# First values of a decoder trunk from unsplit float32 products, with g_mix transposed ahead of x

## The chip, the core and the metric

The kernel runs on one core of a Trainium2 chip. The metric is device time in microseconds (us), the median of several executions; lower is better. A difference counts here when it is over 0.2% of the time, 0.69 us.

## The reference, cut to what matters

One layer of a decoder trunk works on 256 rows x of 1024 floats, all in float32: a mixer with four head groups (a, b, c, d), a cross-attention into 256 memory rows (mem), a squared-ReLU MLP (1024 to 4096 to 1024) and a last RMSNorm.

```
h = rmsnorm(x, g_mix);  proj = h @ w_in            # w_in: 1024 x 2816
aq, ak, av, bq, bk, bv, cq, ck, cv, dq, dk, dv = split(proj)
y = concat(dilated(aq, ak, av), stick(bq, bk, bv), sliding(cq, ck, cv), moba(dq, dk, dv))
x = x + (group_norm(y) * g_group) @ w_out
x = x + cross_attention(rmsnorm(x, g_cross), rmsnorm(mem, g_mem))
x = x + square(relu(rmsnorm(x, g_mlp) @ w_up)) @ w_down
return rmsnorm(x, g_final)
```

The change touches the very first product, `av`: 256 rows times 256 columns of `w_in`, contracted over 1024.

## The kernel before

**Tiles.** The 256 rows are two blocks of 128, x0 and x1 (t = 0, 1). The 1024 features are eight blocks of 128 (k). A weight unit is 1024 x 256 and comes in two halves of 512 KB (k 0 to 3 and 4 to 7).

**Split products.** TensorE (PE) multiplies in the type that the rows call fp32r, so that an operand is split in two: ScalarE (ACT) copies it to the rounded form (hi, L314 for weights, L400 for activations) and VectorE (DVE) subtracts that from the whole (lo, L315, L401). A product then is three (hi·hi, hi·lo, lo·hi: L424 to L426). Weights land in four `raw` buffers; a raw buffer is free again when its L315 has run.

**The front.** SyncE (SP) loads x0, half 0 of av, x1, half 1 of av, then the units aq, ak and so on; ACT's queue loads g_mix, 8 x 128 floats (`grow`). PE multiplies a zero tile by itself 40 times (L366, the warm-ups). For each block of rows, `gained_T` transposes eight 128 x 128 pieces of x on PE (L407), DVE multiplies them by the gains gT (L417, into `tmp`) and the result is split into hThi (L400) and hTlo (L401). gT comes from one small transpose of g_mix (L375) and a copy (L376). `rstd_row` squares x with a sum on ACT (L392), DVE scales the sum (L385, `var`), and GpSimd (POOL) raises it to -1/2 (L386, `rstd`). The two rstd columns are spread over the partitions by two PE transposes (L459) and copied to rk and rq (L462, L463).

The values of group a are 48 products (L495): for each block of rows and each half of the features, hi·hi, lo·hi and hi·lo. After them on PE come the units aq and ak (48 products each, L424 to L426), the scores (L637), and all else. The bias strip of group a goes through DRAM: L471 (PE), L472 (DVE), a store (L473) and three broadcast loads (L717), both issued by POOL.

**Order.** The program is not issued as written. Each operation is handed to a planner (`Plan`) with an estimated price; the planner runs all engines forward on these prices, takes at each step the operation that it ranks highest among those that can start, and emits them in that order. So every engine works through a fixed queue, and an instruction that waits holds all behind it. A changed price or dependence can move instructions far from the change.

Of the kernel before, what the change touches and what calls it, by code (L numbers as in the profile page):

```python
# [11 lines left out]
F32 = mybir.dt.float32  # L12
# [6 lines left out]
P = 128  # L19
S = 256  # L20
D = 1024
KB = D // P
# [4 lines left out]
SPL = 15  # L27
# [4 lines left out]
FRONT = 20.0  # L32
EARLY = 1.0
NUDGE = 0.5
LAST = 2
SPLIT = 640
LASTC = 768
# [178 lines left out]
def trunk(ctx: ExitStack, tc: tile.TileContext, a: dict, out: bass.AP):  # L216
    nc = tc.nc
# [7 lines left out]
    def buf(tag, shape, dtype=F32, bufs=1, pool=sb):  # L225
        return Buf(plan, pool, shape, dtype, tag, bufs)

    def pst(n=1):
        return buf("ps", [P, 512], F32, 4, ps)

    def acct():
        return buf("acc", [P, 512], F32, 4, ps)


    def act(n, fn, r, w, aps=0):
        plan.add("ACT", 0.02 + n * 0.00093 + 0.1 * aps, fn, r, w)

    def dve(n, fn, r, w, rate=1.05):
        plan.add("DVE", 0.065 + n * rate * 1e-3, fn, r, w)
# [9 lines left out]
    def pe(cost, fn, r, w):  # L249
        plan.add("PE", cost, fn, r, w)  # L250

    def dma(nbytes, fn, r, w):
        plan.add("DMA", max(0.06, nbytes / 360e3), fn, r, w)
# [9 lines left out]
    def tsl(t):  # L263
        return slice(t * P, (t + 1) * P)

    def nsl(n):
        return slice(n * 512, (n + 1) * 512)
# [14 lines left out]
    units = {}  # L282
# [10 lines left out]
    def load(u, *which):  # L293

        n, c = units[u].shape[1] // 2, units[u].shape[2]
        got = parts.setdefault(u, ([], n))[0]
        for part in which or range(2):
            raw = buf("raw", [P, n, c], F32, RAW)
            hi, lo = buf("w", [P, n, c], F32R, SPL), buf("w", [P, n, c], F32R, SPL)
            dma(n * c * 512, lambda raw=raw, part=part: nc.sync.dma_start(raw.t, units[u][:, part * n:(part + 1) * n]), [], [raw])  # L300
            if u == "cq":
                def view(z, r):
                    return z.t[:, :, tsl(r)].rearrange("p k (g e) -> p k g e", g=2)

                def src(z, r):
                    return z.t.rearrange("p k (g r e) -> p k r g e", g=2, r=2)[:, :, r]

                for r in range(2):
                    act(512, lambda raw=raw, hi=hi, r=r: nc.scalar.activation(view(hi, r), src(raw, r), AF.Copy),
                        [raw], [(hi, r)])  # L310
                    dve(512, lambda raw=raw, hi=hi, lo=lo, r=r: nc.vector.tensor_sub(
                        view(lo, r), src(raw, r), view(hi, r).bitcast(F32)), [raw, (hi, r)], [(lo, r)])
            else:
                act(1024, lambda raw=raw, hi=hi: nc.scalar.activation(hi.t, raw.t, AF.Copy), [raw], [hi])  # L314
                dve(1024, lambda raw=raw, hi=hi, lo=lo: nc.vector.tensor_sub(lo.t, raw.t, hi.t.bitcast(F32)), [raw, hi], [lo])  # L315
            got.append((hi, lo))

    def wt(u, k):

        got, n = parts[u]  # L320
        return got[k // n], k % n


    xt = []
# [1 line left out]
        xt.append(buf(f"x{t}", [P, D]))  # L326

    def load_x(t):
        dma(P * D * 4, lambda: nc.sync.dma_start(xt[t].t, a["x"][0, tsl(t), :]), [], [xt[t]])

    GN = ("g_mix", "g_cross", "g_mem", "g_mlp")
    grow = [buf("grow0", [KB, P]), buf("grow1", [3 * KB, P])]
# [1 line left out]
    def load_gain(i, eng):  # L334
        j = max(i - 1, 0) * KB
        dma(4096, lambda: eng.dma_start(
            grow[i > 0].t[j:j + KB, :], a[GN[i]][0].rearrange("(k p) -> k p", p=P)), [], [(grow[i > 0], i)])

    load_x(0)
    load_gain(0, nc.scalar)  # L340
    load("av", 0)
    load_x(1)
    load("av", 1)
    ident, mhalf, warm = buf("ident", [P, P]), buf("mhalf", [P, 1]), buf("warm", [P, 512], BF16)
    pool(0.5, lambda: make_identity(nc, ident.t), [], [ident])
    pool(0.05, lambda: nc.gpsimd.memset(mhalf.t, -0.5), [], [mhalf])
# [48 lines left out]
    def pair(tag, n, bufs):  # L395
        return tuple(buf(tag + x, [P, n, S], F32R, bufs) for x in ("hi", "lo"))

    def split_to(hl, key, sl, src, view, n):
        hi, lo = hl
        act(n, lambda: nc.scalar.activation(hi.t[sl], view(), AF.Copy), [src], [(hi, key)])  # L400
        dve(n, lambda: nc.vector.tensor_sub(lo.t[sl], view(), hi.t[sl].bitcast(F32)), [src, (hi, key)], [(lo, key)])  # L401

    def transpose(dst, src, view, n, keys):

        def go():
            for k in range(n):
                nc.tensor.transpose(dst[:, tsl(k)], view()[:, tsl(k)], ident.t)  # L407
        pe(0.109 * n, go, [ident] + keys, [dst])

    def gained_T(x, g, hl, t):  # L410

        tmp = buf("tmp", [P, KB, P], F32, 3)
        for n in range(2):
            ks = slice(4 * n, 4 * n + 4)
            pt = pst()
            transpose(pt, x, lambda n=n: x[:, nsl(n)], 4, [(x, n)])
            dve(512, lambda ks=ks, pt=pt: nc.vector.tensor_tensor(  # L417
                tmp[:, ks, :], pt.t.rearrange("p (k t) -> p k t", k=4), gT[g > 0][:, max(g - 1, 0), ks, None].to_broadcast([P, 4, P]),
                op=ALU.mult), [pt, gT[g > 0]], [(tmp, n)])
            split_to(hl, (t, n), (slice(None), ks, tsl(t)), (tmp, n), lambda ks=ks: tmp[:, ks, :], 512)  # L420

    def mm3(dst, l, r, start, stop):
        (lh, ll), (rh, rl) = l, r
# [22 lines left out]


    h1 = pair("hT", KB, 2)
    r1 = []
    for t in range(2):  # L450
        gained_T(xt[t], 0, h1, t)
        r1.append(rstd_row(xt[t], lambda t=t: xt[t].t, D))

    rq, rk = buf("rq", [P, S]), buf("rk", [P, S])
# [21 lines left out]
    def project(gi):  # L476
        n = "abcd"[gi]
        q, k = buf("q", [P, 2, S], F32, 2), buf("k", [P, 2, S], F32, 2)
        names = (n + "q", n + "k" if gi != 2 else "ckv")
        v = buf("v4", [P, 2, 4, E + 1], F32, 2) if gi != 2 else buf("v2", [P, 2, 2, E + 1])  # L480
        pool(0.1, lambda: nc.gpsimd.memset(v[:, :, :, E:E + 1], 1.0), [], [(v, 0), (v, 1)])

        def values():
            if gi:
                load(n + "v")
            for t in range(2):
                pv = acct()
                if gi:
                    proj(pv, lambda pv=pv: pv[:, 0:256], n + "v", h1, t)
                else:  # L490
                    for half in range(2):
                        for p in ((0, 0), (1, 0), (0, 1)):
                            for kk in range(4 * half, 4 * half + 4):
                                w, j = wt("av", kk)
                                pe(0.109, lambda p=p, kk=kk, w=w, j=j, t=t, pv=pv: nc.tensor.matmul(  # L495
                                    pv[:, 0:256], h1[p[0]][:, kk, tsl(t)], w[p[1]][:, j], start=kk == 0 and p == (0, 0),
                                    stop=kk == KB - 1 and p == (0, 1)), [w[p[1]], (h1[p[0]], (t, half))], [pv])
                act(256, lambda t=t, pv=pv: nc.scalar.activation(
                    v[:, t, :, 0:E], pv[:, 0:256].rearrange("p (h e) -> p h e", h=4), AF.Copy, scale=r1[t].t),
                    [pv, r1[t]], [(v, t)], 1)  # L500

        if gi == 0:
            values()
        for u, z, r in zip(names, (q, k), (rq, rk)):
            if u != "aq":
                load(u)
            acc = acct()
            for i in range(2):
                proj_T(acc, lambda acc=acc, i=i: acc[:, i * S:(i + 1) * S], u, i, h1)
            dve(512, lambda z=z, r=r, acc=acc: nc.vector.tensor_tensor(  # L510
                z.t, acc.t.rearrange("p (i t) -> p i t", i=2), r[:, None, :].to_broadcast([P, 2, S]), op=ALU.mult),
                [acc, r], [z])
        if gi == 2:
            pt = pst()
            transpose(pt, k, lambda: k[:, 1, :], 2, [k])
            for t in range(2):
                act(128, lambda t=t: nc.scalar.activation(
                    v[:, t, :, 0:E], pt[:, tsl(t)].rearrange("p (g e) -> p g e", g=2), AF.Copy), [pt], [(v, t)])
        elif gi:
            values()  # L520
        return q, k, v
# [238 lines left out]
    for t in range(2):  # L760
        pv = pst()
# [12 lines left out]
    for t in range(2):  # L774
        plan.nudge = NUDGE * (1 - t)
        residual(pacc[t], t)
# [10 lines left out]
        w, nm = buf("w4", [P, 4, S], F32, 2), buf("nm", [P, 4], F32, 4)  # L787
# [62 lines left out]
    p = {}  # L850
# [114 lines left out]
    for f, i in enumerate(final):  # L965
        load(("down", i))
        if f < len(final) - LAST:
            for t in range(2):
                for acc, c0, c1 in pieces[t]:
                    rows_mm(acc, hid[i], ("down", i), t, c0, c1, f == 0 and acc not in p.values(), False)  # L970
    for t in range(2):
        o, x = buf("tmp", [P, KB, P], F32, 3), xt[t]
        ssq, pre, var = buf("ssq3", [P, 4], F32, 2), buf("ssq", [P, 1], F32, 4), buf("var", [P, 1], F32, 4)
        sq, r = buf("sq", [P, D], BF16, 1), buf("rstd", [P, 1], F32, 16)
        for c, (acc, c0, c1) in enumerate(pieces[t]):
            cs, n = slice(c0, c1), c0 // 512
            for i in final[-LAST:]:
                rows_mm(acc, hid[i], ("down", i), t, c0, c1, i == final[0] and acc not in p.values(), i == final[-1])
# [67 lines left out]
```

## Time and profile before

| | us |
|---|---|
| three runs | 342.67, 343.07, 343.04 |
| median | 343.04 |
| the profiled execution | 342.83 |
| its span, first to last instruction | 340.9 |

The profiled execution is 0.21 us under the median, and 1.93 us of it lie outside its span. PE is busy 97% of the span, DVE 88%, ACT 68%, POOL 8%. The views name an instruction by its line, engine and out<-in tiles; "busy" of PE includes a modelled end of each product, so that products that start 0.12 us apart are shown 0.28 us long.

### The profile page before, as it was taken

How to read it: one execution, taken by the hardware profiler on the slowest of the kernel's cores; microseconds unless marked ns; L12 is line 12 of the kernel's file. 1: busy time of each engine (PE TensorE's matmuls, PEld its weight loads, DVE VectorE, ACT ScalarE, POOL GpSimd, SP SyncE). 2: the span in 40 equal slices, each digit the busy share in tenths (PEclk: the TensorE clock that was granted, in tenths of full speed). 3: DMA queues.
4: the chain of work that ended last, by engine and by line, in shares of the span. 5: the costliest groups of instructions: out<-in, count | busy, mean ns of one | idle time of the engine just before them, and what ended most of it. 6: DMA issues, size and time to landing. Idle time of an engine off the chain costs nothing.

```text
span 340.9 us, 6081 instructions
## 1 busy us (share of the span) xinstructions
PE 329.0 (97%) x2326; PEld 302.4 (89%) x2326; DVE 299.2 (88%) x488; ACT 231.7 (68%) x371; POOL 27.6 (8%) x46
## 2 busy tenths in 40 slices
PE   7799999999999999999999999999999999999992
PEld 6699899999898789998998899888999889998882
DVE  3758779779998499878999999999999999999994
ACT  4578857369794476883885876778668678665822
POOL 6422000000121002200020000000000000000000
PEclk9999999999999999999999999999999999999997
DMA  7989775640137334847743646476566574644003
GB/s 257 317 254 330 218 201 181 236 137 0 64 109 214 112 122 147 268 143 227 268 139 109 222 160 232 147 229 198 178 225 211 178 248 159 212 123 125 3 0 123
DMA packets 39757, 59.88 MB, mean 176 GB/s; under 512 B 1990, under 2 KB 32896, under 8 KB 39728
## 3 DMA queue, kind: packets, MB, share of 16 engines
q1 hardware_dynamic: 38928, 57.49, 52.2%
q0 software_dynamic: 640, 1.80, 1.8%
q8 instruction: 18, 0.29, 0.4%
q10 hardware_dynamic: 160, 0.20, 0.2%
q14 instruction: 11, 0.09, 0.1%
HBM read 58.42 MB, written 1.07 MB: 175 GB/s over the span
## 4 chain that ended last, share of the span: by engine, by line
PE 57%; DVE 21%; ACT 7%; issue 7%; DMA 5%; POOL 1%; SPq 0%; POOLq 0%; ACTq 0%; DVEq 0%
PE ps L425 9%; PE ps L424 9%; PE ps L426 9%; PE acc L424 8%; PE acc L425 8%; PE acc L426 8%; DVE w L315 5%; DVE w L872 4%; DMA raw<-in_w_in_dram 3%; PE ps L557 3%; PE ps L407 3%; DMA x<-in_x_dram 2%; ACT w L314 2%; DVE tmp L878 2%; POOL rstd L386 1%
## 5 line engine op out<-in xcount | busy, mean ns | idle before, releaser
L315 DVE TENSOR_TENSOR w<-raw,w 128x1024 fp32r<-128x1024 f32 x72 | 86.1, 1218 | 11.6 <-ACT w L314 8.2
L314 ACT ACTIVATE w<-raw 128x1024 fp32r<-128x1024 f32 x72 | 73.9, 1053 | 14.8 <-PE acc L425 7.6
L425 PE MATMUL ps<-hTlo,w 128*128 128x256 f32 x256 | 72.1, 281 | 0.0
L424 PE MATMUL ps<-hThi,w 128*128 128x256 f32 x256 | 71.9, 281 | 0.0
L426 PE MATMUL ps<-hThi,w 128*128 128x256 f32 x256 | 71.8, 281 | 0.0
L424 PEld LDWEIGHTS ps<-hThi,w 128*128 128x128 f32 x256 | 48.2, 188 | 0.7
L425 PEld LDWEIGHTS ps<-hTlo,w 128*128 128x128 f32 x256 | 48.1, 188 | 0.6
L426 PEld LDWEIGHTS ps<-hThi,w 128*128 128x128 f32 x256 | 48.3, 189 | 0.0
L424 PE MATMUL acc<-w,yThi 128*128 128x512 f32 (+1 forms) x112 | 45.2, 404 | 0.0
L425 PE MATMUL acc<-w,yThi 128*128 128x512 f32 (+1 forms) x112 | 43.7, 390 | 0.0
L426 PE MATMUL acc<-w,yTlo 128*128 128x512 f32 (+1 forms) x112 | 43.7, 390 | 0.0
L871 ACT ACTIVATE w<-tmp 128x1024 fp32r<-128x1024 f32 x28 | 29.6, 1058 | 15.6 <-DVE tmp L881 13.1
L424 PE MATMUL acc<-hThi,w 128*128 128x256 f32 x128 | 36.6, 286 | 0.0
L425 PE MATMUL acc<-hTlo,w 128*128 128x256 f32 x128 | 36.1, 282 | 0.0
L426 PE MATMUL acc<-hThi,w 128*128 128x256 f32 x128 | 35.8, 280 | 0.0
L872 DVE TENSOR_TENSOR w<-tmp,w 128x1024 fp32r<-128x1024 f32 x28 | 34.1, 1218 | 0.0
L386 POOL TENSOR_TENSOR rstd<-var,mhalf 128x1 f32<-128x1 f32 x16 | 15.9, 998 | 137.5 <-DVE var L385 89.4
L426 PEld LDWEIGHTS acc<-w,yTlo 128*128 128x128 f32 x112 | 21.0, 188 | 5.0
L425 PEld LDWEIGHTS acc<-w,yThi 128*128 128x128 f32 x112 | 21.1, 188 | 4.2
L424 PEld LDWEIGHTS acc<-w,yThi 128*128 128x128 f32 x112 | 21.1, 188 | 4.0
L424 PEld LDWEIGHTS acc<-hThi,w 128*128 128x128 f32 x128 | 24.1, 188 | 0.4
L426 PEld LDWEIGHTS acc<-hThi,w 128*128 128x128 f32 x128 | 24.2, 189 | 0.0
(189 smaller groups left out, 708.6 us busy)
## 6 DMA issues: line engine op xcount, KB each, us to landing
raw<-in_w_up_dram SPq DMA_DIRECT2D x32, 512.0 KB, 4.2
raw<-in_w_in_dram SPq DMA_DIRECT2D x22, 512.0 KB, 4.9
hThi<-in_w_down_dram SPq DMA_DIRECT2D x14, 512.0 KB, 3.4
hTlo<-in_w_down_dram SPq DMA_DIRECT2D x14, 512.0 KB, 4.1
raw<-in_w_out_dram SPq DMA_DIRECT2D x8, 512.0 KB, 3.4
raw<-in_w_xkv_dram SPq DMA_DIRECT2D x4, 512.0 KB, 3.5
raw<-in_w_down_dram SPq DMA_DIRECT2D x4, 512.0 KB, 4.3
w<-dstrip POOLq DMA_DIRECT2D x3, 512.0 KB, 8.3
```

The source lines that it names most:

```text
L314: act(1024, lambda raw=raw, hi=hi: nc.scalar.activation(hi.t, raw.t, AF.Copy), [raw], [hi])
L315: dve(1024, lambda raw=raw, hi=hi, lo=lo: nc.vector.tensor_sub(lo.t, raw.t, hi.t.bitcast(F32)), [raw, hi], [lo])
L386: pool(0.5, lambda: nc.gpsimd.tensor_tensor(r.t, v.t, mhalf.t, op=ALU.pow), [v, mhalf], [r])
L407: nc.tensor.transpose(dst[:, tsl(k)], view()[:, tsl(k)], ident.t)
L424: nc.tensor.matmul(dst, lh, rh, start=start, stop=False)
L425: nc.tensor.matmul(dst, lh, rl, start=False, stop=False)
L426: nc.tensor.matmul(dst, ll, rh, start=False, stop=stop)
L557: nc.tensor.matmul(view()[:, h, :], z[:, i, :], v[:, j, kv(h), :], start=j == 0, stop=j == len(pT[h]) - 1)
L871: act(512 * n, lambda: nc.scalar.activation(hi.t, view(), AF.Copy), [key], [hi])
L872: dve(512 * n, lambda: nc.vector.tensor_sub(lo.t, view(), hi.t.bitcast(F32)), [key, hi], [lo])
L878: dve(1024, lambda: nc.vector.tensor_sub(s.t, raw[:, 1:2].to_broadcast([P, 2, 512]), raw[:, 0:4:3]), [raw], [s])
```

## The change

The unit av is loaded whole into two tiles of the weight pool (`whole`), not through `raw`, and is not split any more. `gained_T` hands back `tmp`, x transposed and multiplied by the gains in full float32, and the values are 16 products of it with `whole`, float32 by float32, instead of 48 split ones. The 2 copies L314 and 2 subtractions L315 of av are gone; x's own split stays, since aq and all later units use it. The load of g_mix is written first. The load of x1 is given a planned price 1.75 times as large, so that the planner thinks that it lands later; the load itself is the same.

```diff
+FULL = 0.43
     def load_x(t):
-        dma(P * D * 4, lambda: nc.sync.dma_start(xt[t].t, a["x"][0, tsl(t), :]), [], [xt[t]])
+        dma(P * D * (4 + 3 * t), lambda: nc.sync.dma_start(xt[t].t, a["x"][0, tsl(t), :]), [], [xt[t]])
...
+    whole = []
+
+    def load_whole(part):
+
+        whole.append(buf("w", [P, KB // 2, 256], F32, SPL))
+        dma(P * D * 4, lambda: nc.sync.dma_start(whole[part].t, units["av"][:, 4 * part:4 * part + 4]), [], [whole[part]])
+
+    load_gain(0, nc.scalar)
     load_x(0)
-    load_gain(0, nc.scalar)
-    load("av", 0)
+    load_whole(0)
     load_x(1)
-    load("av", 1)
+    load_whole(1)
...
             split_to(hl, (t, n), (slice(None), ks, tsl(t)), (tmp, n), lambda ks=ks: tmp[:, ks, :], 512)
+        return tmp
...
-    r1 = []
+    g1, r1 = [], []
     for t in range(2):
-        gained_T(xt[t], 0, h1, t)
+        g1.append(gained_T(xt[t], 0, h1, t))
...
-                    for half in range(2):
-                        for p in ((0, 0), (1, 0), (0, 1)):
-                            for kk in range(4 * half, 4 * half + 4):
-                                w, j = wt("av", kk)
-                                pe(0.109, lambda p=p, kk=kk, w=w, j=j, t=t, pv=pv: nc.tensor.matmul(
-                                    pv[:, 0:256], h1[p[0]][:, kk, tsl(t)], w[p[1]][:, j], start=kk == 0 and p == (0, 0),
-                                    stop=kk == KB - 1 and p == (0, 1)), [w[p[1]], (h1[p[0]], (t, half))], [pv])
+                    for kk in range(KB):
+                        pe(FULL, lambda kk=kk, t=t, pv=pv: nc.tensor.matmul(
+                            pv[:, 0:256], g1[t][:, kk, :], whole[kk // 4][:, kk % 4], start=kk == 0, stop=kk == KB - 1),
+                            [whole[kk // 4], (g1[t], kk // 4)], [pv])
```

The new order is seen best around the two spread transposes. PE before, from the middle of the values to the first product of aq (`acc_209` is the value sum of x1, `acc_194` that of x0, `rstd_248` belongs to x1, `acc_291` to aq):

```order
L495 MATMUL acc_209<-w_147,hTlo_204 128x256 x2
L495 MATMUL acc_209<-w_173,hThi_163 128x256 x3
L459 MATMUL ps_261<-ident_65,rstd_175 128x128
L459 MATMUL ps_261<-ident_65,rstd_248 128x128
L495 MATMUL acc_209<-w_173,hThi_163 128x256
L495 MATMUL acc_209<-w_215,hThi_163 128x256 x4
L495 MATMUL acc_209<-w_215,hTlo_204 128x256
L495 MATMUL acc_194<-w_252,hThi_163 128x256 x4
L495 MATMUL acc_209<-w_215,hTlo_204 128x256 x3
L495 MATMUL acc_209<-w_252,hThi_163 128x256 x3
L424 MATMUL acc_291<-hThi_163,w_228 128x256
```

PE of the changed kernel at the same place (L501 is the new product, L468 the spread, L480 the bias strip, L433 aq; `acc_147` is x0's sum, `acc_229` x1's):

```order
L501 MATMUL acc_147<-w_166,tmp_134 128x256
L480 MATMUL ps_201<-q_73,rel_87 13x384
L501 MATMUL acc_147<-w_166,tmp_134 128x256
L468 MATMUL ps_211<-ident_65,rstd_156 128x128
L468 MATMUL ps_211<-ident_65,rstd_204 128x128
L501 MATMUL acc_147<-w_166,tmp_134 128x256 x2
L501 MATMUL acc_229<-w_104,tmp_188 128x256 x4
L433 MATMUL acc_245<-hThi_145,w_215 128x256
```

Before, 16 short products stood between the second spread and aq; now 6 long ones do. The first four of x0 (k 0 to 3) have run still earlier, between x0's and x1's transposes. The last four of x1 have left the front: they come after ak, three ahead of the scores and one behind them.

DVE before, from the gains of x1 to the first subtraction of aq's weights (`tmp_141` is x0, `tmp_192` x1; `raw_155` is av, `raw_190` aq):

```order
L417 TENSOR_TENSOR tmp_192<-ps_177,gT_0_137 128x512
L417 TENSOR_TENSOR tmp_192<-ps_185,gT_0_137 128x512
L401 TENSOR_TENSOR hTlo_204<-tmp_141,hThi_163 128x4x128
L401 TENSOR_TENSOR hTlo_204<-tmp_192,hThi_163 128x4x128
L401 TENSOR_TENSOR hTlo_204<-tmp_141,hThi_163 128x4x128
L401 TENSOR_TENSOR hTlo_204<-tmp_192,hThi_163 128x4x128
L385 TENSOR_SCALAR var_242<-ssq_183 128x1
L472 TENSOR_TENSOR k_97<-ps_201,k_97 13x384
L315 TENSOR_TENSOR w_252<-raw_155,w_215 128x1024
L315 TENSOR_TENSOR w_273<-raw_190,w_228 128x1024
```

DVE of the changed kernel there (L425 is the gain product, L409 the split of x, L393 var, L481 the bias strip, L477 a 128 x 4 negation, L316 the weights' split):

```order
L409 TENSOR_TENSOR hTlo_153<-tmp_134,hThi_145 128x4x128 x2
L425 TENSOR_TENSOR tmp_188<-ps_175,gT_0_98 128x512
L425 TENSOR_TENSOR tmp_188<-ps_183,gT_0_98 128x512
L393 TENSOR_SCALAR var_199<-ssq_181 128x1
L409 TENSOR_TENSOR hTlo_153<-tmp_188,hThi_145 128x4x128 x2
L481 TENSOR_TENSOR k_102<-ps_201,k_102 13x384
L477 TENSOR_SCALAR nsink_222<-sink_143 128x4
L316 TENSOR_TENSOR w_233<-raw_190,w_215 128x1024
```

x1's var stands directly behind x1's gain products now, ahead of the two subtractions of x1, where it stood behind four. The subtraction of av between the bias strip and aq is gone.

On SP the loads of x and av keep their order. The two loads of mem (512 KB each) move from between ak's halves to behind the first half of cq; ACT's squares of mem (L392) and DVE's scaling of it (L741) move with them, from ahead of the scores of group a to behind its last score block. From the MLP's first products on, all engines have the same order in both kernels.

## Rows read from the trace of the kernel before

**Rows 1.** Busy time by stage: stretch, its length, busy us (instructions) per engine.
```profile
core 0: us, PE busy (x) PEld busy (x) DVE busy (x) ACT busy (x) POOL busy (x), PEclk, DMA share, GB/s
18.60:30.00 11.40, 11.40 (x99) 11.40 (x98) 7.94 (x12) 8.09 (x13) 4.23 (x6) 1.00 0.89 269
30.00:40.00 10.00, 9.23 (x79) 8.67 (x78) 8.75 (x26) 8.43 (x18) 0.14 (x1) 1.00 0.88 287
...
70.00:100.00 30.00, 29.48 (x246) 27.76 (x244) 28.30 (x77) 25.43 (x60) 2.56 (x3) 1.00 0.22 71
...
160.00:320.00 160.00, 160.00 (x1077) 146.75 (x1076) 157.73 (x214) 117.35 (x156) 2.91 (x4) 1.00 0.55 184
```

**Rows 2.** Timeline of PE, 9.4 to 19 us: start, length, line, tiles, count, idle before.
```profile
10.45 0.81 PE L471 MATMUL ps<-q,rel 32*13 32x384 f32 x2
13.43 0.87 PE L495 MATMUL acc<-w,hTlo 128*128 128x256 f32 x6
16.59 0.32 PE L459 MATMUL ps<-ident,rstd 128*128 128x128 f32 x1 [1.83 <-POOL rstd L386]
18.64 0.28 PE L424 MATMUL acc<-hThi,w 128*128 128x256 f32 x1
```

**Rows 3.** Timeline of DVE, 5 to 19 us.
```profile
5.81 1.53 DVE L417 TENSOR_TENSOR tmp<-ps,gT 128x512 f32<-128x512 f32 x2 [4.69 <-ACT gT L376]
7.32 1.22 DVE L315 TENSOR_TENSOR w<-raw,w 128x1024 fp32r<-128x1024 f32 x1
9.64 1.29 DVE L417 TENSOR_TENSOR tmp<-ps,gT 128x512 f32<-128x512 f32 x2 [1.11 <-PE ps L407]
10.85 2.49 DVE L401 TENSOR_TENSOR hTlo<-tmp,hThi 128x512 fp32r<-128x512 f32 x4
13.25 0.15 DVE L385 TENSOR_SCALAR var<-ssq 128x1 f32<-128x1 f32 x1
13.31 0.54 DVE L472 TENSOR_TENSOR k<-ps,k 13x384 f32<-13x384 f32 x1
13.78 2.34 DVE L315 TENSOR_TENSOR w<-raw,w 128x1024 fp32r<-128x1024 f32 x2
```

**Rows 4.** Timeline of POOL, whole span: three of the rows of L386.
```profile
7.55 1.41 POOL L386 TENSOR_TENSOR rstd<-var,mhalf 128x1 f32<-128x1 f32 x1 [2.10 <-DVE var L385]
13.48 3.05 POOL L386 TENSOR_TENSOR rstd<-var,mhalf 128x1 f32<-128x1 f32 x1 [4.52 <-DVE var L385]
...
39.86 0.55 POOL L386 TENSOR_TENSOR rstd<-var,mhalf 128x1 f32<-128x1 f32 x1 [12.49 <-DVE var L385]
```

**Rows 5.** Groups of PE by line and shape: count | busy us, mean ns | idle before.
```profile
L495 PE MATMUL acc<-w,hTlo 128*128 128x256 f32 x16 | 2.7, 279 | 0.0
...
L471 PE MATMUL ps<-q,rel 32*13 32x384 f32 x2 | 0.8, 486 | 0.0
```

**Rows 6.** Timeline of PE, 0 to 9.4 us.
```profile
4.27 1.09 PE L407 MATMUL ps<-ident,x 128*128 128x128 f32 x4 [0.36 <-DMA x<-in_x_dram]
...
6.40 1.91 PE L366 MATMUL acc<-warm 128*128 128x128 bf16 x16
8.49 1.23 PE L407 MATMUL ps<-ident,x 128*128 128x128 f32 x5 [0.17 <-DMA x<-in_x_dram]
```

**Rows 7.** The chain that ended last, near 114 us: eight transposes in mid-kernel.
```profile
114.67 0.87 PE ps L407 x8
```

**Rows 8.** DMA queues in the first 3 us: queue, packets, MB, share of 16 engines.
```profile
q10 hardware_dynamic: 16, 0.00, 1.0%
```

**Rows 9.** Timeline of ACT, 3 to 19 us.
```profile
9.59 0.62 ACT L400 ACTIVATE hThi<-tmp 128x512 fp32r<-128x512 f32 x1
...
11.50 2.00 ACT L314 ACTIVATE w<-raw 128x1024 fp32r<-128x1024 f32 x2
```

**Rows 10.** The waits between 20 and 46 us: who waited for whom, us, times, longest.
```profile
DVE yn L692 <- POOL rstd L386: 1.3, 2, 0.7
...
PE ps L557 <- ACT pT L244: 0.8, 1, 0.8
```

## Prediction

> **What bounds the kernel now.** The stages come first [rows 1]. From 18.6 us on PE has no gap that counts: it is busy 11.40 of 11.40 us, then 9.23 of 10, and 160.00 of 160 in the MLP, where DVE, with 157.73, is close behind. The gaps that the busy column admits after 18.6 us are 0.77 us (30 to 40), 0.52 (70 to 100) and 0.50 (150 to 160; its row is not needed here). So the end is the moment at which PE begins its dense work, plus a fixed amount of work, plus those gaps. The clock column says 1.00, the higher of the two levels, for all these stages.
>
> Next, what starts the dense work. The first product of aq starts at 18.64; ahead of it PE sat idle for 1.83 us until POOL's rstd of x1 [rows 2]. That is the last link of a chain, read from its end: rstd ran from 13.48 to 16.53 [rows 4]; var of x1, which it needs, came at 13.25, behind four subtractions of x's split that took from 10.85 to 13.34; those stood behind the gain products of x1, from 9.64 [rows 3]; these waited for the transposes of x1, which started at 8.49, when x1 had landed [rows 6]. No weight was late here: the copies of av's second half and of aq's first ran from 11.50 without a wait for a transfer [rows 9].
>
> One link is far longer than its work. L386 takes 0.55 us where DVE is idle beside it, but 1.41 and 3.05 at the start [rows 4]. The first of these ended at 8.96, 0.42 us after the subtraction L315 beside it (7.32 to 8.54); the second at 16.53, 0.41 us after the end of the two L315 at 16.12 [rows 3, 4]. So POOL stood still under those subtractions and finished 0.4 us after them. The Trainium skill (GPSIMD Engine Reference, section Specifications) says that POOL's SBUF interfaces are shared with VectorE and that a VectorE instruction with two SBUF inputs contends for them. L315 and L401 are of that kind; the trace agrees, with 0.42 and 0.41 us.
>
> **The change, part by part. Work on PE.** A split product of 256 columns takes 0.118 us: six starts in 0.87 us less the last one's 0.279, over five [rows 2, 5]. 48 take 5.7 us. A float32 by float32 product stands in the trace as L471: two records for 384 columns, 0.81 us in all of which the last is 0.486, so one start every 0.324 [rows 2, 5]; for 256 columns that is 0.216, and 0.43 for a product of two records. 16 take 6.9 us: PE gets 1.2 us more work, at the higher clock. The row has 32 rows and 13 columns of weights where these have 128 and 128, so the weight load might show; a transpose with a 128 x 128 load starts every 0.109 us 0.87 over 8 [rows 7], half of 0.216, so I take it as hidden and bound a product by 0.43 and 0.55.
>
> **The clock, and the products of x0.** Up to 8 us the warm-ups of 128 columns start every 0.107 us (1.91 less some 0.31, over 15) and x's transposes every 0.21 (1.09 less 0.45, over 3) [rows 6]; later a product of 256 columns needs 0.118 and a transpose 0.109 [rows 2, 7]. PE runs at half its rate, as at 1.2 GHz, until about 9.4 us, though the clock column shows 1.00 there as well. The change puts four of the long products between x0's and x1's transposes. g_mix is no hindrance: all 16 packets of its queue had started by 3 us [rows 8], so its transpose runs at about 3 and the warm-ups behind it end at 4.3. The eight transposes of x0 end at about 6.2 (8 x 0.21), as before. The first gain product ends at 6.3; four warm-ups; the products start at 6.7. At the lower rate they take 0.86 us each: three end at 9.2, the fourth, speeded up midway, at 9.8. Seven warm-ups at the higher rate, 0.4 us, and x1's transposes start at 10.2 instead of 8.49, a delay of 1.7. They now run at 0.11 instead of partly 0.21, so the first four end at 10.85, where they ended at about 9.6.
>
> **The chain of x1.** Gain products 10.9 to 12.2 (1.29) [rows 3]; var straight behind, 12.1 to 12.25, as its row starts 0.6 us after its forerunner's. The order of DVE saves here the two subtractions of x0, which now run earlier, and the two of x1, which now follow: var is 1.0 us earlier than 13.25 in spite of the delay. rstd starts at 12.35, and the two subtractions of x1, from 12.27 to 13.5 (2 x 0.62), lie over it. Behind them stands the 0.54 us of L472, which reads only one operand from SBUF, so rstd reads there and ends 0.41 us after them, at 13.9; if it slips in between the two, at 13.3. Then the second spread (0.1), six products (6 x 0.43 = 2.6), and aq starts at 16.6, 2.0 us before 18.64. aq's weights are ready: its first copy runs behind hThi of x1, whose two copies of 0.62 end at 12.9 [rows 9], its subtraction behind L472 and a small one, from 14.2 to 15.4 (1.22); the second half's are ready by 17.1, and needed from 18.0.
>
> **What comes back later.** Four products of x1, 1.7 us, now stand behind ak; before, one of 0.12 did. So PE's dense end moves by 2.0 - 1.7 + 0.1 = 0.4 us; with rstd at 13.3 by 1.0; with products at 0.55 instead of 0.43 (ten behind the spread, 1.2 us in all) by -0.8.
>
> **Work taken off ACT and DVE.** Two copies of 1.0 us and two subtractions of 1.2. Neither engine ends last in the front: the cover is PE's value products and the wait for rstd. Priced at nothing; but av's subtraction no longer holds rstd, which is in the sum above.
>
> **Loads.** Without av in the raw buffers, ak's halves are asked for earlier, and mem's 1 MB no longer stands before bq. The late copy that held PE's L557 for 0.8 us [rows 10] has the same place on ACT but its weights come earlier. In return, the two squares and the scaling of mem now fall between the first and the second normalization of group a, near 40 us, where DVE's yn waits for POOL already (1.3 us in two waits) [rows 10]; I bound the two together by -0.8 and +0.9 us and take 0.
>
> **The sum.** 342.83 (340.9 of span and 1.93 around it) less 0.4 is 342.4 us. Against the median of 343.04 that is 0.6 lower; the profiled execution was 0.2 under that median, so I count from it.
>
> **Rivals. The clock rises early** (faster). The products of x0 start at 6.7 where before short warm-ups ran. If the rate doubles by then, four products take 1.7 instead of 3.1 us, x1's transposes start at 8.9, just behind the landing of x1 at 8.44, and the chain is 1.35 us earlier throughout: 341.0. For it: x0's transposes run unbroken now, since the small one of g_mix has left their middle. Against it: what PE does up to 6.2 us is otherwise the same warm-ups and transposes after which, in this trace, the rate was still the lower one.
>
> **rstd is held through aq's split** (slower). If rstd doesn't get its read in the 0.6 us between the subtractions of x1 and aq's first L315, it is held to 15.4 + 0.4 = 15.8, 1.9 us later, and aq's second half, whose copy stands behind rk and rq on ACT, doesn't help. That is 344.3. For it: at 13.48 rstd started beside L472 and still was held through both L315 [rows 3, 4]. Against: there 0.3 us were left of L472, here rstd has been waiting when it starts. It decides if less than about 0.15 us lie free between the subtractions.
>
> **The gain is given back** (between). The moved work on mem delays the second yn beyond what PE has to do meanwhile, at the upper bound of 0.9: 343.3. And if the change doesn't do what it says, because something else than the split work keeps rstd's end at 16.5, then aq starts at 16.6 + 0.1 + 2.6 = 19.3, 0.7 later, and 1.6 more is left behind ak: 345.1. I count that with the held rstd.
>
> **How the numbers follow.** 0.2% is 0.69 us, about what a measurement of this kernel tells from no change. My forecast, 342.4 (own range 341.7 to 343.1), has a chance of 0.50, of which 0.12 lies below 342.14 and next to none over 343.5. The early clock 0.26, all faster. rstd held 0.10, all slower. The gain given back 0.14, half of it slower. Faster is 0.12 + 0.26 = 0.38; slower 0.10 + 0.07 = 0.17; the rest, 0.45, is the same. The range runs from 340.8, the lower edge of the early clock, to 343.7, which leaves out the held rstd and a little at the other end.
>
> **What would show it.** In the profile of the changed kernel: the first long product near 6.7 us and its spacing, 0.86 or 0.43; x1's transposes at 10.2 (8.9 in the first rival); var of x1 at 12.1; rstd ending 0.4 us behind the second hTlo at 13.9, not at 15.8; the first L433 at 16.6; four L501 behind ak, 1.7 us; PE's idle time from 30 to 40 us near 0.8. I am wrong if a long product at the higher clock takes clearly more than 0.43, if x1's chain is bound by something other than PE's four products, or if PE's gaps after 30 us grow by more than 0.7 us.

## The result, and the profile after

The changed kernel takes 345.75 us (345.04 to 346.28), the kernel before in the same series 343.06 (341.97 to 345.61): a ratio of 1.0067, 95% interval 1.004 to 1.0094. By that ratio it is slower by some 2.3 us (2.7 between the medians), against a forecast of 342.4 and a range that ended at 343.7. The profiled execution took 345.80 us with a span of 343.8, 2.9 more than before.

Busy time by stage after the change, in the columns of [rows 1], with one more stage, 150 to 160:

```profile
core 0: us, PE busy (x) PEld busy (x) DVE busy (x) ACT busy (x) POOL busy (x), PEclk, DMA share, GB/s
...
18.60:30.00 11.40, 10.08 (x81) 9.34 (x79) 3.65 (x4) 3.10 (x4) 0.74 (x1) 1.00 1.05 348
30.00:40.00 10.00, 8.45 (x62) 7.26 (x61) 8.68 (x26) 9.67 (x23) 1.07 (x1) 1.00 0.79 254
...
70.00:100.00 30.00, 29.52 (x244) 27.81 (x243) 27.27 (x76) 25.14 (x59) 2.56 (x3) 1.00 0.21 71
...
150.00:160.00 10.00, 8.46 (x67) 7.57 (x66) 7.89 (x14) 6.73 (x15) 0.00 (x0) 1.00 0.56 164
160.00:320.00 160.00, 160.00 (x1077) 146.61 (x1076) 156.88 (x214) 114.89 (x154) 2.91 (x4) 1.00 0.55 184
```

PE now has gaps in two places where it had next to none: 2.87 us between 18.6 and 40 (before 0.77 [rows 1]), and 1.54 between 150 and 160 (before 0.50). ACT and DVE ran under a third of the time in the first stretch, with the DMA engines full. All other stages are as they were, within 0.2 us.

The front itself went better than forecast. PE's timeline, start and length first:

```profile
6.20 1.99 PE L501 MATMUL acc<-w,tmp 128*128 128x256 f32 x8
...
8.42 1.04 PE L415 MATMUL ps<-ident,x 128*128 128x128 f32 x8
...
11.77 2.76 PE L501 MATMUL acc<-w,tmp 128*128 128x256 f32 x12
14.17 0.47 PE L433 MATMUL acc<-hThi,w 128*128 128x256 f32 x1
```

aq starts at 14.17, 4.47 us earlier than the 18.64 of [rows 2], where I had forecast 16.6. What that lead ran into stands on ACT, in the copies of the raw weights (idle time before them and its releaser at the end):

```profile
16.06 1.06 ACT L315 ACTIVATE w<-raw 128x1024 fp32r<-128x1024 f32 x1 [0.35 <-DMA raw<-in_w_in_dram]
19.66 1.06 ACT L315 ACTIVATE w<-raw 128x1024 fp32r<-128x1024 f32 x1 [2.54 <-DMA raw<-in_w_in_dram]
24.88 1.06 ACT L315 ACTIVATE w<-raw 128x1024 fp32r<-128x1024 f32 x1 [4.16 <-DMA raw<-in_w_in_dram]
29.02 1.06 ACT L315 ACTIVATE w<-raw 128x1024 fp32r<-128x1024 f32 x1 [3.08 <-DMA raw<-in_w_in_dram]
```

The first row is ak's second half; the other three are bq's two halves and bk's first. Each was asked for early enough: bk's first half was issued at 17.00 us and landed at 28.91, 11.9 us for 0.5 MB. What held it shows on the DMA queues, first from 22 to 24 us and then from 26 to 28 (queue, packets, MB, share of 16 engines):

```profile
q0 software_dynamic: 146, 0.51, 78.5%
q1 hardware_dynamic: 149, 0.15, 23.5%
```

```profile
q1 hardware_dynamic: 603, 0.60, 94.3%
q0 software_dynamic: 34, 0.09, 13.6%
```

q0 carries the bias tiles that POOL broadcasts from dstrip, three of 0.5 MB; q1 carries the weights. While both are at work each gets as many packets, 146 and 149, but q0's packets hold 3.5 KB and q1's 1.0, so the weights get a quarter of their rate. The Trainium skill (DMA: Bandwidth & Descriptors, section Queues, rings and completion order) says that an engine takes turns between its queues packet by packet; the trace agrees, with 146 to 149. The broadcasts moved because the change moved x1's chain: dstrip's table is finished by DVE's addition behind var of x1, its store stands behind rstd of x1 on POOL's queue, and the broadcasts wait until the store has landed. POOL's timeline shows the store and then the first broadcast, before:

```profile
16.50 0.56 POOL L473 DMA_DIRECT2D dstrip<-k  x1
23.13 0.80 POOL L717 DMA_DIRECT2D w<-dstrip  x1 [6.07 <-DMA dstrip<-k]
```

and after the change:

```profile
10.50 1.06 POOL L394 TENSOR_TENSOR rstd<-var,mhalf 128x1 f32<-128x1 f32 x1 [2.38 <-DVE var L393]
12.49 0.56 POOL L482 DMA_DIRECT2D dstrip<-k  x1 [0.94 <-DVE nsink L477]
16.50 0.80 POOL L723 DMA_DIRECT2D w<-dstrip  x1 [3.45 <-DMA dstrip<-k]
```

Before, the store was issued as rstd of x1 ended. The first broadcast was issued at 23.1 us, now at 16.50, just ahead of bk's first half. Of these 6.6 us the chain gave 4.0; the other 2.6 came from the store, which landed 6.3 us after its issue before and 3.7 now. The loss reaches PE over DVE's queue, where the scaling of q and k stands behind the split of the late bq:

```profile
25.97 1.23 DVE L316 TENSOR_TENSOR w<-raw,w 128x1024 fp32r<-128x1024 f32 x1 [3.99 <-ACT w L315]
27.11 0.68 DVE L516 TENSOR_TENSOR q<-acc,rq 128x512 f32<-128x512 f32 x1
27.71 0.68 DVE L516 TENSOR_TENSOR k<-acc,rk 128x512 f32<-128x512 f32 x1
```

```profile
28.45 0.71 PE L643 MATMUL ps<-k,q 64*128 64x128 f32 x8 [1.32 <-DVE k L516]
```

One mark on PE's way, the 41st transpose of probabilities (L539 before, L545 after), stood at 98.90 us and now stands 1.0 us later; the last but one residual addition of x's second block (161.05 before; the last block ahead of the MLP) stands 2.8 later. So the lead of 4.5 us was a lag of 1.0 by 99 us: of the 5.5 us between, the four products left behind ak are 1.7, and the rest is waiting. Then 1.8 more were lost between 99 and 161. Below, *lag* means these two numbers.

### The profile page after: what moved, and what is told of

Same layout as the page of the kernel before. It is cut to its first block, busy times and chain, and to the rows that moved or that the text cites. A ratio compares the mean times of both kernels' runs of the same rounds, so it can differ in the third digit from the quotient of the medians.

```text
span 343.8 us, 6044 instructions
## 1 busy us (share of the span) xinstructions
PE 330.2 (96%) x2310; PEld 301.2 (88%) x2310; DVE 297.5 (87%) x487; ACT 228.9 (67%) x368; POOL 25.9 (8%) x46
## 4 chain that ended last, share of the span: by engine, by line
PE 67%; DVE 11%; ACT 9%; DMA 6%; issue 3%; SPq 1%; POOL 1%; POOLq 0%; ACTq 0%; DVEq 0%
PE ps L434 11%; PE ps L433 11%; PE ps L435 11%; PE acc L433 9%; PE acc L434 9%; PE acc L435 9%; DMA raw<-in_w_in_dram 6%; DVE w L316 3%; PE ps L563 2%; ACT w L315 2%; PE ps L415 2%; ACT qs L603 2%; ACT ks L591 1%; DVE pT L244 1%; ACT w L683 1%
## 5 line engine op out<-in xcount | busy, mean ns | idle before, releaser
L316 DVE TENSOR_TENSOR w<-raw,w 128x1024 fp32r<-128x1024 f32 x70 | 83.7, 1219 | 15.3 <-ACT w L315 15.2
L315 ACT ACTIVATE w<-raw 128x1024 fp32r<-128x1024 f32 x70 | 71.8, 1050 | 18.9 <-DMA raw<-in_w_in_dram 10.8
L433 PE MATMUL ps<-hThi,w 128*128 128x256 f32 x256 | 72.0, 281 | 0.0
L433 PEld LDWEIGHTS ps<-hThi,w 128*128 128x128 f32 x256 | 48.2, 188 | 0.7
L433 PE MATMUL acc<-w,yThi 128*128 128x512 f32 (+1 forms) x112 | 45.2, 404 | 0.1
L433 PE MATMUL acc<-hThi,w 128*128 128x256 f32 x128 | 36.9, 288 | 0.0
L394 POOL TENSOR_TENSOR rstd<-var,mhalf 128x1 f32<-128x1 f32 x16 | 14.3, 916 | 143.0 <-DVE var L393 98.4
L433 PEld LDWEIGHTS acc<-w,yThi 128*128 128x128 f32 x112 | 21.0, 188 | 4.3 <-PE acc L374 0.2
L434 PEld LDWEIGHTS acc<-w,yThi 128*128 128x128 f32 x112 | 21.1, 188 | 4.1
L433 PEld LDWEIGHTS acc<-hThi,w 128*128 128x128 f32 x128 | 24.1, 188 | 0.5 <-ACT w L315 0.2
```

Source lines behind the costliest of these rows:

```text
L394: pool(0.5, lambda: nc.gpsimd.tensor_tensor(r.t, v.t, mhalf.t, op=ALU.pow), [v, mhalf], [r])
L433: nc.tensor.matmul(dst, lh, rh, start=start, stop=False)
L434: nc.tensor.matmul(dst, lh, rl, start=False, stop=False)
```

## The experiments

All compared with the kernel before on the same chip. The times first, with what turned out to matter: when the first 0.5 MB broadcast was issued, and bk's first half (issue, landing).

| kernel | first broadcast | bk, first half | lag at 99, 161 | median us | ratio to before (95%) |
|---|---|---|---|---|---|
| before | 23.1 | 23.4, 28.8 | 0, 0 | 342.9 to 343.4 | 1 |
| changed | 16.5 | 17.0, 28.9 | +1.0, +2.8 | 345.75 | 1.0067 (1.004 to 1.0094) |
| e1_old_tail | 17.8 | 17.5, 26.0 | -1.9, -1.8 | 341.12 | 0.9942 (0.9924 to 0.996) |
| e2_late_bias | 17.8, one | 16.8, 23.6 | -3.3, -1.7 | 341.86 | 0.9975 (0.9966 to 0.9985) |
| e3_cost327 | 18.5 | 17.6, 24.8 | -2.8, -2.7 | 340.31 | 0.9924 (0.9905 to 0.9944) |
| e4_order_only | 15.8 | 22.9, 30.0 | +2.3, +2.3 | 345.22 | 1.0077 (1.0051 to 1.0103) |
| e5_products_only | 16.5 | 22.6, 30.4 | -0.1, +0.2 | 344.69 | 1.0052 (1.0018 to 1.0085) |
| e6_two_casts_out | 17.1, one | 17.6, 26.2 | -1.6, +0.2 | 343.63 | 1.0008 (0.9977 to 1.004) |
| e7_late_327 | 18.6, one | 17.9, 23.3 | -2.9, -3.1 | 340.28 | 0.9908 (0.9878 to 0.9938) |
| e8_order_late | 15.7, one | 22.2, 27.8 | -0.8, -1.0 | 342.00 | 0.9968 (0.9946 to 0.999) |
| e9_before_late | 21.6, one | 25.6, 29.3 | +0.2, -0.1 | 342.84 | 0.9992 (0.9976 to 1.0008) |
| e10_cost44 | 17.1 | 17.6, 29.1 | +1.3, +1.9 | 344.88 | 1.0046 (1.0021 to 1.007) |
| e11_cost30 | 17.8 | 21.1, 29.9 | -0.3, -0.2 | 342.61 | 0.9971 (0.994 to 1.0002) |
| e12_late_30 | 18.1, one | 17.0, 22.1 | -2.7, -2.9 | 340.26 | 0.9912 (0.9882 to 0.9942) |

("One": only one 0.5 MB broadcast is issued there, the other two later or not at all.)

**Two places of loss, told apart by the planner's prices.** e1 gives the planner another price for x's second block, e3 another price for a plain product. The work is the same. In e3 the order moves already at the front; e1 keeps every engine's order up to 111 us, but for three more warm-ups.

```diff
-        dma(P * D * (4 + 3 * t), lambda: nc.sync.dma_start(xt[t].t, ...
+        dma(P * D * (4 + 4 * t), lambda: nc.sync.dma_start(xt[t].t, ...
```

> Only the planner's price of x's second block is raised further (4 + 4t in place of 4 + 3t). The planner then arranges TensorE, VectorE and ScalarE behind 60 us in the order of the kernel before; the front keeps the plain products and the early order. Theory A (of the 2.9 us that the span grew, some 1.0 is lost ahead of 75 us and some 1.8 between 104 and 155 us, by the other order of the out products, the xq/xkv splits and the residual there): TensorE's lag behind the kernel before stays near +1.0 us from 75 us to the end, 344.0 (343.6 to 344.4). Theory B (the order there does not matter; the front's loss grows as it is handed on): 345.5 to 346.

```diff
-FULL = 0.43
+FULL = 0.327
```

> Only the planner's price of a plain product falls from 0.43 to 0.327 us; the work is the same. The planner's order behind 60 us is then that of the kernel before, and the eight products of x's second block stand ahead of others. Theory A: as with the raised price of x's second block, the 1.8 us between 104 and 155 us go; 343.6 to 344.4, and the front keeps what it has. Theory B (only the true price gives a good front): 345.5 or more, with new stalls ahead of 40 us.

Both ran faster than either theory: 341.12 and 340.31. Theory A's part on the end of the kernel held, since the lag doesn't change between 99 and 161 us where the order there is that of before. But the front did not lose 1.0 us, it won 1.9 and 2.8. In both, bk's first half is issued ahead of the first broadcast, by 0.3 and 0.9 us, where the changed kernel issues it 0.5 us behind. So the front's loss was not a price of the plain products, but of where the broadcasts fell. In e1 not even the order put them there. The store of dstrip was issued at 12.59 (12.49 in the changed kernel) and landed 4.9 us later, not 3.7, so that POOL's first broadcast came later by 1.3 us and bk's first half by 0.45:

```profile
17.76 0.80 POOL L723 DMA_DIRECT2D w<-dstrip  x1 [4.61 <-DMA dstrip<-k]
```

Why the store took longer in e1, no run shows. The times are steady nevertheless: 345.0 to 346.3 us in all eight executions of the changed kernel, 340.2 to 341.5 in six of e1's seven.

**The bytes of the broadcasts.** e2 makes the biases of groups 2 and 3 when their groups come; e6 leaves these two out, with every engine's order unchanged.

```diff
-    bias = {gi: buf("w", [P, 4, S], F32, SPL) for gi in (0, 2, 3)}
+    bias = {0: buf("w", [P, 4, S], F32, SPL)}
...
         if gi in (1, 2):
+            bias[gi + 1] = buf("w", [P, 4, S], F32, SPL)
             toeplitz(gi + 1, 4 * gi, 4)
```

> Two of the three bias tiles of 0.5 MB (groups 2 and 3) are made when their group comes, not all three behind aq, so that their broadcasts leave the stretch of 16 to 24 us; all else as in the changed kernel, its order behind 100 us too. Theory A1 (the broadcasts share the DMA engines with bq and bk): bq's second half lands at 22 to 23 us in place of 24.8, ScalarE's wait for raw weights drops from 10 us in sum to 6 or less, TensorE's stall of 1.5 us at 26.75 shrinks below 0.7, and the time falls by 0.8 to 1.5 us to 344.3 to 345.0. Theory A2 (four raw buffers and the one queue set when the weights come): landings move by under 0.7 us, 345.4 to 346.

```diff
         def go():
+            if gi > 1:
+                nc.gpsimd.memset(bias[gi].t, 0.0)
+                return
             src = dstrip.t
```

> The changed kernel, every engine's order unchanged, with the bias broadcasts of groups 2 and 3 (0.5 MB each) left out: a memset on GpSimd of the same tile stands in their place, so groups 2 and 3 attend without a bias. Theory A1 (the bytes of these two broadcasts delay bq and bk): bq's second half lands by 23 us in place of 24.8, the lag behind the kernel before at 75 us turns from +1.0 to -1.5 to -2.5 as with the late biases, and the 1.8 us between 104 and 155 us are still lost: 341.5 to 343. Rival (the late biases gained by the g_mix, g_group and mem loads that moved with them, not by bytes): 344.5 to 346.

e2 came to 341.86, well below what A1 had asked for, with 4.4 us of lag won at 99. These are not the bytes alone, since e2 also issues bk's first half 0.9 us ahead of the broadcast. e6 is the stricter of the two: there bk stands 0.5 us behind it, as in the changed kernel. Its lag at 99 us is -1.6 against +1.0, though its aq started 0.6 us later (14.78). So 1 MB less in that stretch is worth 2.6 us (2.1 between the medians), and 1.8 are lost again behind, as expected. The time, 343.63, is a little above the 341.5 to 343 I had given it. ACT's wait for raw weights from 14 to 36 us, first in the changed kernel, then in e6 (sum, times, longest):

```profile
ACT w L315 <- DMA raw<-in_w_in_dram: 10.1, 4, 4.2
```

```profile
ACT w L315 <- DMA raw<-in_w_in_dram: 6.8, 4, 3.1
```

e11 and e12 are the same pair at another price. At 0.30 the planner's order behind 60 us is that of before, but bk is issued behind all three broadcasts.

```diff
-FULL = 0.43
+FULL = 0.3
```

> The price of a plain product at 0.30 us, the biases as in the changed kernel. The order behind 60 us is that of the kernel before; ahead of it the bias broadcasts and group a's attention stand elsewhere than at 0.327. Theory A1 (what counts is when the broadcasts are issued against bq's second half and bk): with the issue behind 17.5 us and bq's second half landed by 22.5, 339.8 to 341.2. Rival (0.327 was luck in one order, neighbouring prices spread as widely as 341 to 346): over 342.

(e12: that line and e2's edit.)

> Both cures with the price of a plain product at 0.30 us. Theory A with A1: as with 0.327 and late biases, 339.3 to 340.5, the lag at 75 us -2.8 to -3.6. Rival: over 341.

e11 took 342.61, as its rival had it. A1's conditions were met, with the broadcasts issued from 17.8 and bq's second half landed at 21.5, but its time was not: bk's first half, issued at 21.1, landed at 29.9. A1 had left out a transfer that counts. This one had more against it than taking turns, for from 22 to 24 us e11's only queue with packets is that of the broadcasts:

```profile
q0 software_dynamic: 145, 0.50, 97.7%
```

What kept bk's packets out altogether, no run shows. With the late biases e12 took 340.26, 2.4 us less; there bk's first half is also issued ahead of the broadcast, at 17.0. ACT's wait for raw weights from 14 to 36 us, e11 and then e12:

```profile
ACT w L315 <- DMA raw<-in_w_in_dram: 7.3, 1, 7.3
```

```profile
ACT w L315 <- DMA raw<-in_w_in_dram: 1.8, 4, 0.7
```

**Is it the change or the biases?** The kernel before with late biases:

> The kernel before with only the biases of groups 2 and 3 broadcast when their group comes. There the broadcasts are issued at 23 to 25 us and TensorE's stalls between 24 and 40 us are 1.6 us in sum. Theory A1 (the clash needs the early start; before, the weights are ahead): 342.3 to 343.2, no change or half a microsecond. Rival (the broadcasts cost before as well, and the late biases are simply a better kernel): 341 to 342.

342.84, no difference in time. But this doesn't show that the crowding cost nothing, since the edit changed DVE's order too. In e9 aq starts 0.7 us earlier and the wait of 0.77 us after 30 us is gone, while PE has two new waits, at 25.6 us for the split of ak's weights, which stands behind the scaling of mem, and at 94.6:

```profile
PE acc L426 <- DVE w L315: 1.6, 1, 1.6
PE ps L604 <- ACT pT L244: 1.4, 1, 1.4
```

What bounds the cost of the crowding in the kernel before is PE's own idle time from 18.6 to 70 us, 0.77 us in all (30 to 40 us in [rows 1]); in the changed kernel it is 3.0. So the clash needs the early start, by the trace of before rather than by e9.

**The end of the kernel.** e10 raises the price by 0.01. Up to 130 us its order is that of the changed kernel, but for one warm-up.

```diff
-FULL = 0.43
+FULL = 0.44
```

> The changed kernel with the planner's price of a plain product at 0.44 in place of 0.43 us. Up to 130 us every engine's order is that of the changed kernel, but for one warm-up less; behind it VectorE's split of xo no longer stands between the two minima of the cross attention of x's first block, and the scores of one block stand ahead of two transposes. Theory A (the stall of 1.32 us at 150.01 comes from that split): the lag stays +1.0 at 75 and +1.7 at 140, and ends at +1.5 to +1.9 in place of +2.8; 344.3 to 344.9. Rival (the split has to be made anyhow and stalls TensorE elsewhere): 345.5 to 346.

DVE around the two minima L802 of the cross attention of x's first block, in the changed kernel:

```profile
146.33 0.69 DVE L802 TENSOR_REDUCE nm<-ps 128x2 f32<-128x512 f32 x1
146.94 1.22 DVE L316 TENSOR_TENSOR w<-raw,w 128x1024 fp32r<-128x1024 f32 x1
148.92 0.69 DVE L802 TENSOR_REDUCE nm<-ps 128x2 f32<-128x512 f32 x1 [0.76 <-PE ps L611]
```

PE's wait from 145 to 152 us there:

```profile
PE ps L545 <- ACT w L807: 1.2, 1, 1.2
```

and DVE in e10:

```profile
146.57 1.29 DVE L802 TENSOR_REDUCE nm<-ps 128x2 f32<-128x512 f32 x2
147.78 1.22 DVE L316 TENSOR_TENSOR w<-raw,w 128x1024 fp32r<-128x1024 f32 x1
```

In the changed kernel a split of 1.22 us stands ahead of the second minimum, because PE makes the second block of scores only behind two transposes; the exponentials wait, and PE waits for them, 1.2 us. In e10 the wait is gone, and the lag between 99 and 161 us grows by 0.6 instead of 1.8. The time fell to 344.88, at the upper edge of what theory A gave. The remaining 0.6 builds up between 103 and 128 us, where out's products, the splits and the residual stand in another order. e1, which has the changed kernel's order up to 111 us and behind it that of before, loses nothing between 99 and 161; but its front ran 2.9 us ahead, so the 0.6 is not shown by itself.

**Order without products, products without order.** e4 and e8 take the two order edits alone, with av's products split as before; e5 takes the plain products alone.

```diff
-        dma(P * D * 4, lambda: nc.sync.dma_start(xt[t].t, ...
+        dma(P * D * (4 + 3 * t), lambda: nc.sync.dma_start(xt[t].t, ...
...
+    load_gain(0, nc.scalar)
     load_x(0)
-    load_gain(0, nc.scalar)
```

> The kernel before with two parts of the change alone: g_mix is loaded ahead of x's first block, and x's second block is priced at 7 bytes an element. The products of av stay split, 48 short ones. If the early clock and the early transposes come from this order alone: the clock rises at about 5.5 us, aq starts at 15 to 16.5 us, later than 14.2 since av's splits are on ScalarE and VectorE again. Theory A (what is won ahead of aq is given back where bq and bk are waited for): 342.6 to 343.6, no change. Theory C (the plain products cost the time, 1.2 us more of TensorE, not the order): 341 to 342.

(e8: that and e2's edit.)

> The kernel before with split products, with the two order edits (g_mix first, x's second block at 7 bytes) and with the biases of groups 2 and 3 broadcast when their group comes. Theory A1 (the order alone lost 2.3 us since the broadcasts stood ahead of bq and bk): most of that comes back, 341.8 to 343.2. Rival (av's splits on ScalarE and VectorE hold aq's and ak's, and the early order needs the plain products): 344.5 to 345.5.

> The changed kernel with the two order edits taken back: x's first block is loaded ahead of g_mix again and x's second block is priced at 4 bytes an element; the plain products stay. Its order between 100 and 113 us is neither that of before nor that of the changed kernel. Theory (the products are worth having, what decides is when the bias broadcasts meet bq and bk): the broadcasts' issue and the landing of bq's second half tell the result; with broadcasts ahead of 17 us and bq's second half behind 24 us 344 to 346, with broadcasts later 341 to 343. Rival (g_mix ahead of x is what starts the clock at 5.5 us): the clock rises at 8 us or later here and aq starts 1 to 3 us later than 14.2.

Neither theory on e4 held: it took 345.22, as slow as the changed kernel. aq starts as early as 14.78 although av is split; but the broadcasts are issued from 15.8 us, bq's first half lands at 27.0, and PE stands 2.2 us ahead of its first scores. With late biases (e8) the time is 342.00, so most of that loss was the clash here too, with some 1.3 us of it from the lower clock that followed PE's wait (an estimate; the last section has its rows). The order edits alone are enough to bring aq forward: with the order of before and a clock that rose earlier still, aq starts at 17.93 (e9). The plain products alone are enough as well: without the order edits (e5) aq starts at 14.20. The clock rose early there too, so the rival of e5 falls. Its broadcasts came at 16.5, bq's second half landed in time (20.9), bk at 30.4; 344.69 is in the band for early broadcasts. Its lag is only 0.2 at 161 us; another 0.8 comes in the last 30 us, for which I have no cause.

**Both cures.** e2's edit with the price 0.327:

> The changed kernel with the planner's price of a plain product at 0.327 us and with the biases of groups 2 and 3 broadcast when their group comes: both cures together. Theory A with A1: ahead of 75 us the lag behind the kernel before is -3.0 to -3.6 us, a little better than -2.8 with the price alone, since the stalls of 24 to 40 us there sum to only 0.8; behind 100 us nothing is lost: 339.3 to 340.3. Rival (with the price alone the clash is already gone and the later broadcasts of 49 and 73 us meet other loads): 340.3 to 341.2.

340.28, the upper end of A's band, and the same as e3 within the error: with bk ahead of the broadcasts the clash is nearly gone, as the rival had it. The late biases also come with a wait of their own. PE's only wait from 14 to 100 us in e7 is at 91.5:

```profile
PE ps L610 <- ACT pT L245: 1.4, 1, 1.4
```

e8, e9 and e12 have it too, e2 one of 0.7; the kernels with early biases have 0.3 there. No run tests where it comes from. The stages of e7, to set beside those of the changed kernel:

```profile
core 0: us, PE busy (x) PEld busy (x) DVE busy (x) ACT busy (x) POOL busy (x), PEclk, DMA share, GB/s
...
18.60:30.00 11.40, 11.40 (x98) 11.10 (x97) 5.67 (x7) 5.13 (x8) 1.34 (x2) 1.00 1.01 305
30.00:40.00 10.00, 10.00 (x85) 9.49 (x84) 8.80 (x30) 9.94 (x23) 1.21 (x3) 1.00 0.59 189
...
150.00:160.00 10.00, 9.55 (x58) 7.95 (x57) 8.43 (x15) 4.38 (x8) 0.00 (x0) 1.00 0.75 243
```

PE has no gap from 18.6 to 40 us, and 0.45 from 150 to 160. e3, e7 and e12 beat both kernels, the one before by 0.8 to 0.9%. The split products with early order and late biases (e8) stand 1.7 us above e7 and e12, measured in another series; that difference holds for these orders, since I have no pair that differs in the products alone.

## Why the prediction was wrong, by its steps

- **The plain product**, 0.43 us: right. Twelve records of L501, two to a product, start 0.216 us apart from 11.77 to 14.15, and aq follows at 14.17.
- **The clock, and the products of x0**: too late. The rate had doubled by 5.5 us, the products ran from 6.20 at 0.43, not 0.86, and x1's transposes started at 8.42, not 10.2. The first rival had the mechanism, and was still late at 8.9, since it let x1 land at 8.44; it landed at 7.44.
- **The chain of x1**: var at 10.27 instead of 12.1; rstd from 10.50 to 11.56, where it slips in between the two subtractions (10.45 to 11.75). It ended 0.42 us behind the end of the first one, as in [rows 4], though no time lies free between the two. Why the rstd of before was held through both of two such subtractions is open. That was the branch I gave half a sentence, "if it slips in between the two". Held through aq's split it was not: that rival falls.
- **Six products behind the spread, 2.6 us, then aq**: right (twelve records, 2.4). **Four left behind ak, 1.7 us**: right, eight records between 25.67 and 29.79.
- **The sum of the front**: 342.83 less 4.47, plus 1.6 for what is left behind, would be 340.0. In e3, e7 and e12, in which neither loss occurs, aq starts later, at 15.72, 15.38 and 15.89, and two, two and one products are left behind. The same sum gives 340.7, 340.3 and 340.4; they ran at 340.3. The reading that PE's start sets the end was sound; it could be cashed only where the weights kept up.
- **Loads: the step that failed.** I followed mem and ak's halves past bq, bounded the effect by 0.8 and 0.9 and took it at nothing. Measured, PE waited 3.8 us on the way from 14 to 99 us (the 5.5 lost there less 1.7 for the four products). I did not follow what hangs on var and rstd of x1 besides the spread: the addition L481 on DVE, the store of dstrip behind rstd, and three broadcasts on POOL's queue. They moved forward with the chain that I had moved myself, by 6.6 us, into the time in which bq and bk load. Two of the three cost 2.6 us (e6); making them late in another order, with bk ahead of the one that is left, gave 2.4 (e12 against e11). What is open is what sets, within one order, whether bk or the broadcast is first (e1).
- **mem's squares and the second yn**: of no weight. DVE waits 0.9 us for POOL's rstd ahead of yn, 1.3 before [rows 10]. The third rival's place was wrong, though its kind, a gain given back to a late transfer, was right.
- **"A fixed amount of work, plus those gaps"**: failed a second time behind 100 us. The planner's order depends on its own clock, and a front arranged otherwise changed the order of instructions that the diff does not touch. That cost 1.8 us, 1.2 of it removed by 0.01 us in a price. The order of both kernels was there to be compared ahead of time; I compared it only at the front.
- **What would make it wrong**: the third of my conditions came true. PE's gaps after 30 us grew by more than 0.7 us, in 30 to 40 from 0.77 to 1.55 and in 150 to 160 from 0.50 to 1.54.

## What to carry to other kernels

When a chain is moved forward, list everything that hangs on it, also the small operation that lets a large transfer go; a broadcast that comes early can cost more than the wait it ends. Where a planner sets the order, compare its order to the very end, and try its prices. The order does not fix which of two queues gets to the DMA engines first, as e1 shows. As for prices, here one constant that changes no work spread the time from 340.3 (e3) to 345.75 us. A gain at the front is worth its face only if the next stage's data are ahead of it.

## What the runs showed of the hardware

**TensorE's instructions don't fix when the clock rises.** The kernel before and e9 have the same TensorE instructions in the same order in the front. In [rows 6] sixteen warm-ups from 6.40 take 1.91 us. In e9, on PE's timeline:

```profile
4.17 0.63 PE L407 MATMUL ps<-ident,x 128*128 128x128 f32 x4 [0.25 <-DMA x<-in_x_dram]
...
5.38 1.06 PE L366 MATMUL acc<-warm 128*128 128x128 bf16 x16
```

Sixteen take 1.06 us, and x's transposes already run at the higher rate from 4.2 us. Over all fourteen profiles, one to a kernel, the rate doubled between 3.9 and 9.5 us, the latest in the one execution from which I forecast. In e9 aq started 0.7 us earlier; what that is worth at the end isn't shown, as e9 has waits that the kernel before has not.

**The clock can fall again in mid-kernel.** In e4 PE stood 2.2 us ahead of its first scores. The granted clock by stretch there:

```profile
core 0: us, PE busy (x) PEld busy (x) DVE busy (x) ACT busy (x) POOL busy (x), PEclk, DMA share, GB/s
30.00:33.10 3.10, 0.89 (x11) 0.69 (x11) 2.41 (x4) 3.10 (x4) 0.00 (x0) 1.00 0.67 181
33.20:36.50 3.30, 3.30 (x18) 3.08 (x17) 3.17 (x12) 2.38 (x7) 0.00 (x0) 0.50 0.85 194
36.60:40.00 3.40, 3.40 (x32) 3.40 (x31) 2.28 (x10) 2.07 (x5) 0.00 (x0) 1.00 1.01 360
```

In the 3.1 us with this wait PE was busy for 0.89. Then it was granted 0.50, the lower level, for 3.3 us, and ran 18 records in them where the next 3.4 us hold 32. Fourteen of the 18 are products that start 0.21 us apart where later ones start 0.12 apart, which cost some 1.3 us (an estimate). In the changed kernel the longest wait was 1.3 us, in the kernel before 1.83 [rows 2], and the clock stayed at 1.00 in both.
